# Six chunks of a K-split projection and their conditioning products: another order for the conditioning visits

## The chip, the cores and the metric

The kernel runs on one core of one Trainium2 chip. The metric is device time in microseconds: 1735.44 is the median of three runs (1734.55 to 1738.17).

## The reference, cut to what matters

One decoder layer is computed in float32 for 256 prompt rows and 8 x 4 sample rows, so 288 rows of width 2048, and nine conditioning vectors (one prompt, eight samples).

```python
mod = (jax.nn.silu(c) @ w_ada + b_ada).reshape(N, 1, N_MOD, D)
sh1, sc1, g1, sh2, sc2, g2 = [mod[:, :, i] for i in range(N_MOD)]
h = rmsnorm(x, norm1) * (1 + sc1) + sh1
proj = h @ w_in                       # 2048 -> 10752
...                                   # three gated branches, merged
x = x + g1 * (merged @ w_out)
h2 = rmsnorm(x, norm2) * (1 + sc2) + sh2
x = x + g2 * (jnp.square(jax.nn.relu(h2 @ w_ff1)) @ w_ff2)
```

`proj` cannot start before `sh1` and `sc1` are there for the rows of `h` that it contracts over. Both are products of the conditioning vectors with 2048 x 2048 blocks of `w_ada`, 33.6 MB together.

## The kernel before, in words

Activations lie transposed: 2048 features are 16 tiles of 128 partitions, with 288 columns (rows of x) each. A weight matrix is read in **pieces** of 256 x 512 float32 (512 KB, class `Piece`, load in L246). A piece is split into a high and a low part in a format that TensorE takes at speed (L256 on ScalarE, then L257 on VectorE), and 24 matmuls follow for it (L265 to L267: four blocks of 128 outputs, two k tiles, three products).

All loads of weights go through nine buffers of 512 KB (`rawp`, RAW = 9), in the order of the program, on the queue of SyncE. A buffer of a piece is free once both its splits are done.

The **conditioning visits** (class `AdaFirst`, loads in L146, matmuls in L162) compute `sh1` and `sc1` for a chunk of feature tiles. `ada_first(t0, nt)` makes, for the nt tiles from t0 on, 2 visits where nt is 2 and 4 visits where nt is 4 (two steps each, `per=2`). Each visit has four loads of 512 KB (their rows are 1 KB where nt is 2 and 2 KB where nt is 4) and holds its four buffers until its matmuls are done. The last visit of a chunk is followed by `finish`: the result is copied (L167, ScalarE), transposed (L175, TensorE), summed (L178 and `mod_rows`, VectorE), and `modulated` (L410 to L432, VectorE and ScalarE in turn) makes the two parts of h for this chunk. It is written at a higher priority than the code around it.

The first eight groups of `w_in` (512 outputs each) contract over h in six **chunks** of k tiles, (0,2), (2,2), (4,2), (6,2), (8,4), (12,4). A chunk of two tiles has one piece of each group, so 8 pieces; one of four tiles has 16. So the pieces p0 to p63 in order are: chunk 0 = p0 to p7, chunk 1 = p8 to p15, chunk 2 = p16 to p23, chunk 3 = p24 to p31, chunk 4 = p32 to p47, chunk 5 = p48 to p63. Partial sums are added on VectorE (L303). The visits for chunks 1 to 5 are 2 + 2 + 2 + 4 + 4 = 14, here numbered v0 to v13; v1, v3, v5, v9 and v13 are the last ones of their chunks. Those of chunk 0 (`a0`, eight loads) come ahead of p0.

The list `items` gives the order, and `drive` walks it: before the matmuls of an item it issues the splits of the next two items, and loads as far ahead as nine buffers go. In the kernel before, the visits for chunk c + 1 stand among the pieces of chunk c: L965 puts v0 ahead of p2 and v1 ahead of p5; `interleave` spreads the others over the next chunks, so that v2, v4, v6, v10 stand ahead of the first piece of their stretch, and v9 is three pieces ahead of p32. The visits in the pieces of chunk 3 are v6 ahead of p24, v7 ahead of p26, v8 ahead of p27 and v9 ahead of p29. Among the pieces of chunk 5 and later stand the visits of class `Ada` for the other four parts of `mod` (L203, L215).

Three calls lie in the list too: `load_consts` with `mask_consts` (six loads on SyncE's queue; work on GpSimd) ahead of p26, `prep_states` (transposes L520, L524) ahead of p35, and `prep_sgu` (L511) ahead of p38.

Of the kernel before, what the change touches and what calls it, by code (L numbers as in the profile page):

```python
# [32 lines left out]
def decoder_step(ctx: ExitStack, tc: tile.TileContext, A: dict, O: dict):  # L33
# [151 lines left out]
    def ada_first(t0, nt, per=2):  # L185
        s_ = {}
        return [AdaFirst(s_, t0, nt, list(range(i, i + per))) for i in range(0, 2 * nt, per)]
# [95 lines left out]
    def group(src, n0, kts, rhs, done, krow0=0, width=T):  # L283
        st = {}
        np_ = len(kts) // 2
        return [Piece(st, src, krow0 + i * 256, n0, kts[2 * i:2 * i + 2], rhs, i == 0, i == np_ - 1, done, width)
                for i in range(np_)]

    def chunked(src, n0, rhs, done, chunks):

        part = {}
        last = len(chunks) - 1

        def gather(c):
            def fn(ps):
                if c == 0:
                    part["t"] = atile(F32, (P, 4, T))
                t = part["t"]
                for b in range(4):
                    if c == 0:  # L300
                        S.copy(out=t[:, b, :], in_=ps[b])
                    else:
                        V.tensor_add(out=t[:, b, :], in0=ps[b], in1=t[:, b, :])  # L303
                if c == last:
                    return done([t[:, b, :] for b in range(4)], t)
            return fn

        return [group(src, n0, list(range(t0, t0 + nt)), rhs, gather(c), krow0=t0 * P)
                for c, (t0, nt) in enumerate(chunks)]
# [146 lines left out]
    def x_blocks(b0, b1, move):  # L456
        for b in range(b0, b1):
            acc = bankA()
            for tt, (halves, rows) in enumerate(xs):
                st["pe"] = PE.transpose(out=acc[:, tt * P:tt * P + rows],  # L460
                                        in_=halves[b // 8][:rows, (b % 8) * P:(b % 8 + 1) * P],
                                        identity=ident[:rows, :rows]).ins
            move(out=X[b // 4][:, b % 4, :], in_=acc[:, 0:T])
# [203 lines left out]
    def done_cc(h):  # L667
        def done(ps, _):
            z = gtile((P, 4, WC))
            zs = z[:, :, 2 + TP:WC].rearrange("p b (n k) -> p b n k", k=6)  # L670
            V.memset(z[:, :, 0:2], 0.0)
            for b in range(4):
                G.tensor_copy(out=zs[:, b, :, 0:2], in_=scT[:, 4 * h + b, :].rearrange("p (n k) -> p n k", k=2))
                V.tensor_mul(out=z[:, b, 2:2 + TP], in0=ps[b][:, 0:TP], in1=st["xc"][:, b, 0:TP])
                V.tensor_mul(out=zs[:, b, :, 2:6], in0=ps[b][:, TP:T].rearrange("p (n i) -> p n i", i=TS),
                             in1=st["xc"][:, b, TP:T].rearrange("p (n i) -> p n i", i=TS))
            cv = gtile((P, 4, WC))
            L = WC - 2
            for b in range(4):
                wk = [wcT[:, k * 8 + 4 * h + b:k * 8 + 4 * h + b + 1] for k in range(3)]  # L680
                S.mul(out=cv[:, b, 0:L], in_=z[:, b, 0:L], mul=wk[0])
                V.scalar_tensor_tensor(out=cv[:, b, 0:L], in0=z[:, b, 1:1 + L], scalar=wk[1], in1=cv[:, b, 0:L],
                                       op0=ALU.mult, op1=ALU.add)
                V.scalar_tensor_tensor(out=cv[:, b, 0:L], in0=z[:, b, 2:2 + L], scalar=wk[2], in1=cv[:, b, 0:L],
                                       op0=ALU.mult, op1=ALU.add)
            st["cv", h] = cv
            zt = sp.tile([P, 4, 18], F32, tag="zt", name="zt", bufs=1)
            G.tensor_copy(out=zt[:, :, 0:2], in_=z[:, :, TP:TP + 2])
            for b in range(4):
                G.tensor_copy(out=zt[:, b, 2:18].rearrange("p (n k) -> p n k", k=2), in_=zs[:, b, :, 4:6])  # L690
            return [(4, lambda: conv_tail(h, zt))]
        return done
# [11 lines left out]
    def done_bc(h):  # L704
        def done(ps, _=None):
            cv = st["cv", h]
            cs = cv[:, :, TP:WC - 2 + 0].rearrange("p b (n k) -> p b n k", k=6)
            y = gtile()
            for b in range(4):
                V.tensor_mul(out=y[:, b, 0:TP], in0=ps[b][:, 0:TP], in1=cv[:, b, 0:TP])  # L710
                V.tensor_mul(out=y[:, b, TP:T].rearrange("p (n i) -> p n i", i=TS),
                             in0=ps[b][:, TP:T].rearrange("p (n i) -> p n i", i=TS), in1=cs[:, b, :, 2:6])
            BR[1 + h] = split_act(y)
        return done
# [124 lines left out]
    def done_ff2(q4, j):  # L839
        def done(ps):  # L840
            for b in range(4):
                residual(X[j], j, b, ps[b], 5)
            if q4 < 3:
                return
            add_squares(j)
            xf = gtile()
            for b in range(4):
                S.mul(out=xf[:, b, :], in_=X[j][:, b, :], mul=fnT[:, 4 * j + b:4 * j + b + 1])

            def out_t():  # L850
                for t_, (c0, n) in enumerate(TILES):
                    tp = bankB()
                    for b in range(4):
                        PE.transpose(out=tp[:n, b * P:(b + 1) * P], in_=xf[:, b, c0:c0 + n], identity=ident)  # L854
                    if j % 2 == 0:
                        Y[t_][j // 2] = atile(F32, (P, 1024))
                    (V.tensor_copy if t_ % 2 else S.copy)(out=Y[t_][j // 2][:n, (j % 2) * 512:(j % 2 + 1) * 512],
                                                          in_=tp[:n])
            return [(3, out_t)]
        return done  # L860
# [60 lines left out]
    def interleave(main, extra, tail):  # L921

        out, n, done = [], len(main) - tail, 0
        for i, x in enumerate(main):
            while done < len(extra) and done * n <= i * len(extra):
                out.append(extra[done])
                done += 1
            out.append(x)
        return out + extra[done:]


    chunks = [(0, 2), (2, 2), (4, 2), (6, 2), (8, 4), (12, 4)]
    first = [(OFF_V, done_v), (OFF_XC, done_xc), (OFF_CC, done_cc(0)), (OFF_BC, done_bc(0)), (OFF_U, done_u),
             (OFF_P, done_p), (OFF_XC + 512, done_xc), (OFF_CC + 512, done_cc(1))]
    first = [chunked(w_in, n0, rhs_h, dn, chunks) for n0, dn in first]
    a0 = ada_first(*chunks[0], per=1)
    fill = []
# [3 lines left out]
    def queued(fn):  # L941

        def run():
            with tc.issue_after(st["pe"]):
                return fn()
        return run
# [6 lines left out]
    for it in a0:  # L953
        it.mm = queued(it.mm)
    items = [Call(x_early), a0[0], Call(queued(lambda: x_blocks(7, 9, V.tensor_copy))), a0[1],
             Call(queued(prep_vec)), Call(x_stats), a0[2],
             Call(queued(lambda: x_blocks(9, 10, V.tensor_copy))), a0[3],
             Call(queued(lambda: x_blocks(10, 13, S.copy))), Call(queued(lambda: x_blocks(13, KT, V.tensor_copy)))]
    for c in range(len(chunks)):
        ps_ = [x for g_ in first for x in g_[c]]  # L960
        ex = ada_first(*chunks[c + 1]) if c + 1 < len(chunks) else fill[0:4]
        if c == 0:
            for it in ex:
                it.mm = queued(it.mm)
        mix = ps_[0:2] + ex[0:1] + ps_[2:5] + ex[1:2] + ps_[5:] if c == 0 else interleave(ps_, ex, 2)  # L965
        if c == 3:
            mix = mix[:4] + [Call(mask_consts, load_consts)] + mix[4:]
        if c == 4:
            mix = mix[:4] + [Call(prep_states)] + mix[4:8] + [Call(prep_sgu)] + mix[8:]
        items += mix  # L970

    main = []
    main += group(w_in, OFF_BC + 512, K16, rhs_h, done_bc(1))
# [26 lines left out]
    for q4 in range(4):  # L1000
# [3 lines left out]
        for j in range(4):  # L1004
            g_ = group(w2, j * 512, K16, rhs_f, done_ff2(q4, j), krow0=q4 * D)
# [36 lines left out]
```

## Time and profile before

| what | value |
|---|---|
| median of three runs | 1735.44 us |
| the profiled execution: time, span | 1735.38 us, 1733.6 us |
| TensorE busy | 1703.1 us, 98% |
| VectorE, ScalarE, GpSimd busy | 903.9, 666.5, 135.7 us |
| read from HBM | 360.58 MB, 210 GB/s over the span |

Times in the rows are microseconds from the start of the span. A busy TensorE is one with a matmul under way. The chain of waits is followed back from the last instruction; each row is a stretch of it, with its start, its length, and the engine, tile and line that it spent the time in. Loads of weights are seen in two ways: their issues on SyncE's queue (where the length of a row holds the waiting for buffers between its issues) and the rate of the DMA engines by slices of time.

### The profile page before, as it was taken

What the parts mean: (1) busy time and instruction counts of PE and PEld (TensorE: products, weight loads), DVE (VectorE), ACT (ScalarE), POOL (GpSimd) and SP (SyncE); (2) the same over time, 40 slices, a digit from 0 to 9 for tenths busy, and PEclk for the clock granted to TensorE, in tenths of its full rate; (3) what the DMA queues carried; (4) which work ended last, traced back from release to release, by engine and by line L of the source; (5) the groups of instructions that cost most, each with busy time, mean ns of one, the idle gap of its engine ahead of it and who ended that gap; (6) DMA issues with size and microseconds to landing.
All of it is one profiled execution on the core that took longest, in us unless ns stands there. A gap on an engine that the chain in (4) does not pass through costs nothing.

```text
span 1733.6 us, 30410 instructions
## 1 busy us (share of the span) xinstructions
PE 1703.1 (98%) x12842; PEld 1615.3 (93%) x12842; DVE 903.9 (52%) x1243; ACT 666.5 (38%) x806; POOL 135.7 (8%) x209
## 2 busy tenths in 40 slices
PE   7999999999999999999999999999999999999997
PEld 4997888999999999999999999999999999999997
DVE  3676679534444344455659444445444444445444
ACT  4523344333333333333435333344333443344443
POOL 1000105100000000011310000000000000000011
PEclk9999999999999999999999999999999999999998
DMA  9999876677667766766676645554455544555431
GB/s 301 325 303 327 297 257 227 220 244 238 220 234 255 241 223 230 247 237 225 225 254 234 206 170 160 169 163 166 164 165 170 162 168 164 165 164 165 164 128 55
DMA packets 180847, 365.42 MB, mean 211 GB/s; under 512 B 11932, under 2 KB 29476, under 8 KB 180703
## 3 DMA queue, kind: packets, MB, share of 16 engines
q1 hardware_dynamic: 179735, 362.89, 63.1%
q8 instruction: 100, 1.64, 0.4%
q0 software_dynamic: 976, 0.59, 0.1%
q14 instruction: 36, 0.29, 0.0%
HBM read 360.58 MB, written 3.04 MB: 210 GB/s over the span
## 4 chain that ended last, share of the span: by engine, by line
PE 96%; DVE 1%; DMA 1%; ACT 0%; SPq 0%; issue 0%; POOL 0%; DVEq 0%; ACTq 0%; POOLq 0%
PE acc L265 30%; PE acc L267 30%; PE acc L266 30%; PE misc L215 3%; PE misc L162 2%; DMA raw<-in_w_ada 1%; DVE wl L257 0%; DMA raw<-in_w_in 0%; PE misc L854 0%; PE acc L460 0%; DVE act L897 0%; SPq L72 0%; PE misc L175 0%; ACT wh L256 0%; PE misc L649 0%
## 5 line engine op out<-in xcount | busy, mean ns | idle before, releaser
L265 PE MATMUL acc<-act,wh 128*128 128x288 f32 (+1 forms) x3904 | 1160.0, 297 | 3.3 <-ACT wh L256 2.8
L267 PE MATMUL acc<-act,wl 128*128 128x288 f32 (+1 forms) x3904 | 1154.9, 296 | 3.0 <-DVE wl L257 3.0
L266 PE MATMUL acc<-act,wh 128*128 128x288 f32 (+1 forms) x3904 | 1154.6, 296 | 0.0
L257 DVE TENSOR_TENSOR wl<-raw,wh 128x1024 fp32r<-128x1024 f32 x488 | 619.9, 1274 | 675.4 <-ACT wh L256 674.2
L256 ACT CAST wh<-raw 128x1024 fp32r<-128x1024 f32 x488 | 512.0, 1050 | 950.8 <-PE acc L266 833.4
L265 PEld LDWEIGHTS acc<-act,wh 128*128 128x128 f32 x3904 | 735.9, 189 | 39.4 <-ACT wh L256 26.7
L267 PEld LDWEIGHTS acc<-act,wl 128*128 128x128 f32 x3904 | 736.6, 189 | 3.9 <-DVE wl L257 3.5
L266 PEld LDWEIGHTS acc<-act,wh 128*128 128x128 f32 x3904 | 736.4, 189 | 0.2
L443 POOL TENSOR_TENSOR g<-g,rt 128x32 f32<-128x32 f32 x79 | 34.8, 441 | 861.2 <-DVE rt L441 861.2
L303 DVE TENSOR_TENSOR act<-acc,act 128x288 f32<-128x288 f32 x160 | 68.0, 451 | 31.8 <-PE acc L267 31.3
L215 PE MATMUL misc<-raw,cT 128*32 128x512 f32 x512 | 61.6, 598 | 0.0
L438 DVE SCALAR_TENSOR_TENSOR g<-acc,mod,g 128x256 f32<-128x256 f32 x80 | 38.3, 478 | 44.4 <-PE acc L267 44.4
L736 POOL TENSOR_TENSOR g<-g 128x1152 f32<-128x1152 f32 x8 | 21.3, 2663 | 436.4 <-DVE g L733 436.4
L162 PE MATMUL misc<-raw,cT 128*32 128x256 f32 (+1 forms) x384 | 36.1, 477 | 0.9 <-DMA raw<-in_w_ada 0.9
L215 PEld LDWEIGHTS misc<-raw,cT 128*32 128x32 f32 x512 | 13.4, 109 | 24.2 <-issue 21.4
L371 DVE TENSOR_TENSOR act<-g,act 128x1152 fp32r<-128x1152 f32 (+1 forms) x23 | 35.4, 1540 | 0.6
L733 DVE SCALAR_TENSOR_TENSOR g<-g,acc 128x288 f32<-128x288 f32 x48 | 20.8, 451 | 21.5 <-PE acc L267 21.0
L812 ACT ACTIVATE g<-acc 128x288 f32<-128x288 f32 x56 | 22.8, 408 | 11.0 <-PE acc L267 11.0
L370 ACT CAST act<-g 128x1152 fp32r<-128x1152 f32 (+1 forms) x23 | 26.7, 1161 | 0.9 <-DVE g L650 0.4
L723 ACT ACTIVATE g<-acc 128x288 f32<-128x288 f32 x48 | 19.6, 409 | 12.9 <-PE acc L267 12.9
L162 PEld LDWEIGHTS misc<-raw,cT 128*32 128x32 f32 x384 | 11.4, 113 | 13.7 <-issue 7.5
L813 DVE TENSOR_TENSOR g<-g 128x1152 f32<-128x1152 f32 x14 | 18.9, 1351 | 0.0
(206 smaller groups left out, 400.1 us busy)
## 6 DMA issues: line engine op xcount, KB each, us to landing
raw<-in_w_ff SPq DMA_DIRECT2D x256, 512.0 KB, 3.6
raw<-in_w_ada SPq DMA_DIRECT2D x192, 512.0 KB, 5.8
raw<-in_w_in SPq DMA_DIRECT2D x168, 512.0 KB, 6.1
raw<-in_w_out SPq DMA_DIRECT2D x32, 512.0 KB, 4.2
raw<-in_w_br_conv SPq DMA_DIRECT2D x16, 512.0 KB, 3.7
raw<-in_w_br_pool SPq DMA_DIRECT2D x8, 512.0 KB, 6.2
raw<-in_w_br_sgu SPq DMA_DIRECT2D x8, 512.0 KB, 4.6
act<-in_x_prompt SPq DMA_DIRECT2D x4, 512.0 KB, 7.5
```

The lines of the kernel that those rows point to most:

```text
L162: st["pe"] = PE.matmul(out=acc[32 * j:32 * j + 32, :], lhsT=cT[:, kt, :], rhs=self.w[s, m][:, i, :], start=kt < 2, stop=kt >= KT - 2).ins
L215: PE.matmul(out=acc[32 * j:32 * j + 32, :], lhsT=cT[:, kt, :], rhs=self.w[kt, j // 2][:, (j % 2) * 512:(j % 2 + 1) * 512], start=kt == 0, ...
L256: S.copy(out=self.wh, in_=self.w)
L257: V.tensor_sub(out=self.wl, in0=self.w, in1=self.wh.bitcast(F32))
L265: PE.matmul(out=acc, lhsT=self.wh[:, i, bs], rhs=xh, start=f, stop=False)
L266: PE.matmul(out=acc, lhsT=self.wh[:, i, bs], rhs=xl, start=False, stop=False)
L267: st["pe"] = PE.matmul(out=acc, lhsT=self.wl[:, i, bs], rhs=xh, start=False, stop=l).ins
L303: V.tensor_add(out=t[:, b, :], in0=ps[b], in1=t[:, b, :])
L370: S.copy(out=hi, in_=src)
L371: V.tensor_sub(out=lo, in0=src, in1=hi.bitcast(F32))
L438: V.scalar_tensor_tensor(out=x[:, b, 0:TP], in0=ps[:, 0:TP], scalar=mod[:, mg, kt, 0:1], in1=x[:, b, 0:TP], op0=ALU.mult, op1=ALU.add)
L443: (eng or G).tensor_add(out=x[:, b, TP:T], in0=x[:, b, TP:T], in1=t)
```

## The change

The fourteen visits v0 to v13 become one list. Ahead of piece n (n below 48) stand all visits whose number d, counted from 0, has 1.5 d + 1.5 <= n. The three calls get fixed places, ahead of p28, p36 and p40. The pieces of chunk 5 with the first four `Ada` visits stay as they were. v0 and v1 keep their fence behind the matmuls issued so far (`queued`).

```diff
-    for c in range(len(chunks)):
-        ps_ = [x for g_ in first for x in g_[c]]
-        ex = ada_first(*chunks[c + 1]) if c + 1 < len(chunks) else fill[0:4]
-        if c == 0:
-            for it in ex:
-                it.mm = queued(it.mm)
-        mix = ps_[0:2] + ex[0:1] + ps_[2:5] + ex[1:2] + ps_[5:] if c == 0 else interleave(ps_, ex, 2)
-        if c == 3:
-            mix = mix[:4] + [Call(mask_consts, load_consts)] + mix[4:]
-        if c == 4:
-            mix = mix[:4] + [Call(prep_states)] + mix[4:8] + [Call(prep_sgu)] + mix[8:]
-        items += mix
+    visits = [it for c in range(1, len(chunks)) for it in ada_first(*chunks[c])]
+    for it in visits[0:2]:
+        it.mm = queued(it.mm)
+    extra = {28: [Call(mask_consts, load_consts)], 36: [Call(prep_states)], 40: [Call(prep_sgu)]}
+    pieces = [x for c in range(len(chunks)) for g_ in first for x in g_[c]]
+    last = 4 * chunks[-1][0]
+    done = 0
+    for n, x in enumerate(pieces[0:last]):
+        items += extra.get(n, [])
+        while done < len(visits) and 1.5 * done + 1.5 <= n:
+            items.append(visits[done])
+            done += 1
+        items.append(x)
+    items += interleave(pieces[last:], fill[0:4], 2)
```

## Rows read from the trace of the kernel before

**Rows 1.** The page: busy time by engine, and the chain by engine
```profile
PE 1703.1 (98%) x12842; PEld 1615.3 (93%) x12842; DVE 903.9 (52%) x1243; ACT 666.5 (38%) x806; POOL 135.7 (8%) x209
...
PE 96%; DVE 1%; DMA 1%; ACT 0%; SPq 0%; issue 0%; POOL 0%; DVEq 0%; ACTq 0%; POOLq 0%
```

**Rows 2.** Chain of waits, 0 to 320 us: start, length, what
```profile
39.43 1.86 PE misc L162 x32
...
92.94 1.86 PE misc L162 x32
...
122.79 1.85 PE misc L162 x16
...
144.81 1.92 PE misc L162 x16
146.76 0.59 ACT ev L167
147.40 0.67 PE misc L175 x4
...
152.16 0.40 PE acc L265
...
153.93 0.36 PE misc L520 x2
...
162.36 1.85 PE misc L162 x14
...
175.15 0.59 PE misc L524 x8
...
186.66 0.44 PE misc L511 x4
...
205.17 1.85 PE misc L162 x16
...
208.03 0.44 PE misc L175 x4
...
223.68 1.85 PE misc L215 x16
```

**Rows 3.** Windows by stage: busy time, count, granted clock, DMA share, GB/s
```profile
123.00:162.00 39.00, 35.48 (x263) 27.69 (x256) 25.89 (x56) 11.63 (x15) 0.64 (x1) 1.00 0.96 332
162.00:224.00 62.00, 62.00 (x471) 55.00 (x473) 40.85 (x71) 19.58 (x23) 5.19 (x12) 1.00 0.85 289
```

**Rows 4.** Timeline of ScalarE, 118 to 166 us: start, length, what
```profile
147.24 1.05 ACT L256 CAST wh<-raw 128x1024 fp32r<-128x1024 f32 x1
```

**Rows 5.** Timeline of VectorE, 118 to 166 us
```profile
152.74 0.28 DVE L432 TENSOR_TENSOR act<-g,act 128x128 fp32r<-128x128 f32 x1
152.94 3.48 DVE L257 TENSOR_TENSOR wl<-raw,wh 128x1024 fp32r<-128x1024 f32 x3
```

**Rows 6.** Timeline of SyncE's queue, 0 to 118 us: the first issues of weights
```profile
4.97 13.39 SPq L146 DMA_DIRECT2D raw<-in_w_ada  x8
18.40 2.62 SPq L246 DMA_DIRECT2D raw<-in_w_in  x2
21.12 5.85 SPq L146 DMA_DIRECT2D raw<-in_w_ada  x4
27.07 3.81 SPq L246 DMA_DIRECT2D raw<-in_w_in  x3
33.82 7.57 SPq L146 DMA_DIRECT2D raw<-in_w_ada  x4
```

**Rows 7.** The visits' load, line 146: time from issue to landing
```profile
DMA to landing us min/median/max: 3.7/6.8/11.8
```

**Rows 8.** DMA rate in 40 slices of 18 to 42 us, 0.6 us each
```profile
GB/s 353 343 350 348 348 345 352 347 353 350 376 387 387 377 369 355 355 350 372 328 340 341 357 350 358 374 386 389 386 389 387 364 357 352 350 323 149 55 14 138
```

**Rows 9.** Windows: 138 to 154 us, and the first 20 us
```profile
138.00:154.00 16.00, 12.48 (x87) 9.14 (x84) 10.99 (x28) 5.98 (x10) 0.00 (x0) 1.00 1.04 386
...
0.00:20.00 20.00, 10.60 (x43) 5.05 (x44) 5.08 (x19) 9.77 (x15) 4.58 (x28) 1.00 0.87 265
```

## The prediction

> **What bounds the kernel now.** I read the page first: TensorE is busy 98% of the span and is 96% of the chain that ended last [rows 1]. So a change of order can only win or lose where TensorE waits. Then the chain by stages, between the first conditioning visit and the first `Ada` visit, which starts chunk 5: 39.43 to 223.68 us [rows 2]. Only this stretch changes its order. What TensorE needs there is found from quiet places. From v13 at 205.17 to 223.68 there lie one visit (1.85), one set of transposes (0.44) and five pieces: (18.51 - 1.85 - 0.44) / 5 = 3.24 us for a piece. The stretch holds p2 to p47, so 46 pieces x 3.24 = 149.0, 14 visits x 1.86 = 26.0, and some 3.2 of transposes (L175 five times, L520, L524 and L511 [rows 2]; small ones estimated at half the four-tile ones): 178.2 us. It took 184.25, so 6.1 are waits. Nearly all of it is in one place, behind v9, at 146.76 to 152.16, and the window 123 to 162 shows it as 3.5 us without any matmul [rows 2, 3]. There `finish` goes ahead of the next piece's split: ScalarE casts that piece at 147.24, but VectorE takes its half of the split only at 152.94, after the last instruction of `modulated` [rows 4, 5]. All the rest of the stretch is bound by TensorE, though the transfers are not far behind: 332 GB/s from 123 to 162, 289 from 162 to 224 [rows 3].
>
> **What the change does.** It is said to put each chunk's last visit three pieces ahead of the chunk. The code doesn't. With two steps in a visit there are 14 visits, and the rule 1.5 d + 1.5 <= n puts v0 ahead of p2, v1 of p3, v2 of p5, v3 of p6, and so on to v9 of p15 and v13 of p21. Chunk 4, for which v9 is the last visit, starts at p32, and chunk 5 at p48: the last visits are 5, 10, 15, 17 and 27 pieces ahead. All fourteen now lie within the first 21 pieces, instead of 38 or so, and the 27 pieces p21 to p47 have none. No matmul, split or load is added or removed; what moves is when the bytes are needed.
>
> **Demand against supply.** Two visits and three pieces repeat. They take TensorE 2 x 1.86 + 3 x 3.24 = 13.4 us and need 2 x 4 + 3 = 11 loads of 524,288 bytes, so 5.77 MB: 430 GB/s. What the DMA engines gave when they had all they could take: 349 GB/s in the first ten slices after 18 us, while the 1 KB rows of chunk 0's visits landed, and 386 over the 16 us from 138 on, with pieces and visits of 2 KB rows [rows 8, 9]. A load is then 1.50 us with 1 KB rows and 1.36 with 2 KB rows. So this stretch turns from bound by TensorE to bound by transfers.
>
> **The sum.** Nine buffers let SyncE's queue run ahead only so far. Before v0's matmuls end at 39.43 + 1.86 = 41.29, the kernel before had issued 8 + 2 + 4 + 3 loads and nearly four more [rows 6]. In the new order the loads are 8 of chunk 0, p0, p1, v0's four, p2, v1's four, which is 19; the 20th (p3) is the first that needs a buffer of v0 and goes out at 41.29. Up to the last load of v13 there are 8 + 21 + 56 = 85, so 66 remain: 16 of them (v2 to v5) with 1 KB rows, 50 with 2 KB rows. The first lands 3.7 us after its issue [rows 7], at 45.0; the 65 behind it take 16 x 1.50 + 49 x 1.36 = 90.6. v13 has landed at 135.6, and its matmuls end at 137.5. TensorE alone would have ended v13 at 39.4 + 19 x 3.24 + 14 x 1.86 + 2 = 129, so the transfers cost some 8 us here.
>
> Then v13's `finish`. In the old place of v13 it cost nothing, since the next pieces had been loaded and split before. Now p21 is the load behind v13's, as p29 was behind v9's, and I take what that cost: 5.40 us from the end of the visit to the full run of the next piece, L175's 0.67 among it [rows 2]. The bounds are 0.8 (p21 lands 1.36 after v13 and needs its cast of 1.05 [rows 4], while the visit took 1.86 of that time; a little for the first low half) and 5.4; I take 5.4, the row with the same order of loads. The same chain behind v1, v3, v5 and v9 is costed at nothing, because TensorE waits for loads there anyway and the queue has other buffers to fill; if that cover is gone, each costs up to 3.5 (two tiles, an estimate from half the work of the 5.4) or 5.4 (v9).
>
> Then 27 pieces x 3.24 = 87.5 and 1.5 for L520, L524 and L511, with loads at a third of what the DMA engines can do. Chunk 5 starts at 137.5 + 5.4 + 87.5 + 1.5 = 231.9 instead of 223.68: 8.2 us later. Behind that the order is the old one, and I see nothing that could give it back: chunk 5 is again TensorE with the same `Ada` visits. The three calls move by one or two pieces, and `load_consts` brings its 1.4 MB at a time when the queue is nearly idle instead of one when it carries 332 GB/s; that is hidden by p22 to p27 and costs nothing. The wait behind v9 in the old place is already within the 184.25.
>
> The profiled execution took 1735.38, with 1733.6 in the span, 0.06 off the median of the runs. 1735.4 + 8.2 = 1743.6.
>
> **Which rate holds.** The rows say that 386 GB/s lasted 16 us. The Trainium skill ("DMA: Bandwidth & Descriptors", Specifications) gives about 358 GB/s as the limit of HBM for one core, and 435 for the fabric. By 358 each of the 66 loads would be 1.46 us, an estimate from that page, the sum some 5 us longer and the time 1748; this trace exceeds that limit by 8%, so I don't follow it, but it has never had to keep its rate for 90 us.
>
> **Rivals.**
> (a) *The rate falls to the lowest of the full slices for the whole stretch*, 349 GB/s. For: nothing in the rows lasts 90 us, and freed buffers can come late. Against: 386 for 16 us. Then 66 x 1.50 = 99 instead of 92, +7.3: 1750.9. (This is the side on which the skill's 358 lies.)
> (b) *Every `finish` is exposed*, since each now stands where the next piece has just landed: 3 x 3.5 + 5.4 more would be 1759 at most; a half of it is covered by the waits for loads, 1751. For: [rows 4, 5]. Against: the transfers keep running meanwhile.
> (c) *v13's finish goes behind the splits*, as it did at 208 us, where five pieces ran on at 3.24. Then 137.5 + 0.8 + 87.5 + 1.5 + 0.4 = 227.7, +4.0: 1739.4; with 390 GB/s over all, 2 less, and no difference can be told.
> (d) *Faster: the transfers keep up*, and only the wait behind v9 is gone. Without any wait the stretch takes 178.2, -6.1: 1729.3, for which 430 GB/s are needed. The point from which it decides is v13 landing at 127.4, where the change is even: 66 loads in 84 us, 413 GB/s, or 390 if (c) holds as well. The rows have slices of 389 but no mean above 386. That the change did what it is said to do, with the visits over all 45 pieces, would give the same time; the code excludes it.
> (e) *The granted clock falls* in the new waits. The first 20 us had TensorE busy for 10.60 only, and 138 to 154 for 12.48 of 16, both at 1.00, the 2.4 GHz level [rows 9]; the new stretch is busier than these. If it fell to half, pieces would take 6.5 us, and five of them would already cost 16: 1760.
>
> **Chances and range.** The forecast (transfers bind, v13's finish shows) 0.50; (a) 0.14; (b) 0.11; (c) 0.16; (d) 0.07; (e) 0.02. Some 0.2% or 3.5 us either way can't be told from no change in this kernel: 1732 to 1739. About two thirds of (c) and a tenth of the forecast end there, so 0.16 for no difference; 0.06 for faster; 0.78 for slower. Range: from 1736.5 (between (c) and even) to 1756 (above (a), within (b)).
>
> **What would show it.** SyncE's queue should show v13's loads issued before 136 us and the DMA engines at 350 to 390 GB/s from 45 to 136 without breaks, then about 165. TensorE should wait for L146's loads ahead of v3, v5, v7 and so on, by one to two microseconds each, and have no visit from about 138 to 231. Chunk 5's first L215 should start near 232 instead of 223.68, and all behind it be later by the same. If the DMA rate has gaps in that stretch, the buffers bind and not the engines; if L215 starts before 222, the supply was more than I allow, and the prediction is wrong at its root.

## The result, and the profile after

The changed kernel takes 1753.05 us (median of five runs, 1750.05 to 1756.25) against 1735.44; the ratio is 1.010, 95% interval 1.0087 to 1.0112. It is slower, as forecast, and by 17.6 us instead of 8.2: the time lies inside the range, the loss is twice what was forecast.

First the page of the changed kernel: busy time by engine, and the costliest groups' row of the visits' matmuls (busy us, mean ns of one, idle time before them). Behind it the same row of the kernel before, which had not been shown.

```profile
PE 1714.7 (98%) x12842; PEld 1617.4 (92%) x12842; DVE 904.3 (52%) x1243; ACT 667.3 (38%) x806; POOL 137.0 (8%) x209
...
L162 PE MATMUL misc<-raw,cT 128*32 128x256 f32 (+1 forms) x384 | 43.8, 486 | 0.7 <-DMA raw<-in_w_ada 0.7
```
```profile
L162 PE MATMUL misc<-raw,cT 128*32 128x256 f32 (+1 forms) x384 | 36.1, 477 | 0.9 <-DMA raw<-in_w_ada 0.9
```

The instruction counts are the same, but TensorE is busy for 11.6 us more [rows 1], 7.7 of them in the visits. So not all of the loss is waiting: of the 17.5 us by which the span is longer, 5.9 are. Next the chain of waits of the changed kernel, 0 to 330 us, with v0, v1 and its finish, v7, v9 and its finish, v13, and the first `Ada` visit:

```profile
40.36 1.86 PE misc L162 x32
...
45.62 1.93 PE misc L162 x32
47.63 0.38 ACT ev L167
...
49.29 0.88 DVE g L418 x2
...
51.37 1.15 DVE wl L257
52.56 0.40 PE acc L267
...
97.97 0.97 PE misc L162 x2
101.27 1.85 PE misc L162 x14
...
116.12 1.91 PE misc L162 x14
118.05 0.59 ACT ev L167
...
120.25 1.67 DVE g L418 x4
...
124.12 1.14 DVE wl L257
125.30 0.40 PE acc L267
...
149.62 1.91 PE misc L162 x14
...
242.38 1.85 PE misc L215 x16
```

Read it from behind. Chunk 5 starts at 242.38 instead of 223.68 [rows 2]; from there to the end of the span the two kernels need 1508.7 and 1509.9 us, so everything happens before it. v13 is over at 151.5, and v0 starts at 40.36: 111.2 us, in which TensorE has 89.6 us of work at the prices of the prediction. The window of this way (its length, then TensorE's busy time; the last three columns are the granted clock, the DMA share and GB/s) has 9.5 us without a matmul, and so 12.1 us more with one than those prices give:

```profile
40.30:151.50 111.20, 101.70 (x787) 72.60 (x786) 58.89 (x126) 35.11 (x62) 0.00 (x0) 1.00 0.95 332
```

What stands between is not a wait for the visits' own loads: the chain passes through none of them. Behind v1 and behind v9 it passes through `finish` on VectorE and ScalarE and only then through the low half of the next piece's split (wl): 47.55 to 52.56 and 118.03 to 125.30. In part of that TensorE works on high halves; it is without a matmul for 1.9 us behind v1, 2.5 behind v3, 2.4 behind v5 and 2.5 behind v9, which is nearly all of the 9.5. The next pieces were not late then. The loads of p3 and p4 were issued from 41.40 us on and landed 3.7 and 4.6 us later, ahead of the end of v1 at 47.55; behind v3, v5 and v9 the next piece had landed at 63.2, 81.7 and 114.8, ahead of the visits' ends at 65.6, 84.0 and 118.0. Behind v1 the first of the casts stands on ScalarE behind the copy L167, which waits for the visit (SyncE's row, the landing of its two loads, and two rows of ScalarE):

```profile
41.40 0.88 SPq L246 DMA_DIRECT2D raw<-in_w_in  x2
DMA to landing us min/median/max: 3.7/4.2/4.6
47.63 0.37 ACT L167 COPY ev<-misc 128x256 f32<-128x256 f32 x1 [1.58 <-PE misc L162]
47.90 1.05 ACT L256 CAST wh<-raw 128x1024 fp32r<-128x1024 f32 x1
```

And v7 shows the second thing: its first two records (one matmul) run alone at 97.97, in the middle of a piece, for 0.97 us, and the other 14 at 101.27 for 1.85, what all sixteen take when they run together.

The DMA rate of the changed kernel in 40 slices from 41 to 101 us, 1.5 us each, and the waits of SyncE's queue from 30 to 160 us (line, what it waited for, us in total, times, longest):

```profile
GB/s 16 259 411 338 353 356 352 370 360 345 349 337 132 272 238 320 356 358 354 372 359 350 349 326 136 291 389 306 377 355 389 399 391 385 376 161 15 131 391 400
```
```profile
SPq L246 <- PE misc L162: 39.0, 20, 5.5
SPq L146 <- PE misc L162: 28.9, 8, 6.2
```

The rate is full between, but has a break at 59, at 77 and at 95 us, each behind a last visit (v1, v3, v5) whose finish held TensorE up, and behind v9 one more (46 GB/s from 125 to 126.5 us); the queue stands there for buffers that the next visit's matmuls (L162) have not given back.

### The profile page after: what moved, and what is told of

It reads as the page before. It is cut to its first block, busy times and chain, and to the rows that moved or that the text cites. A ratio compares the mean times of both kernels' runs of the same rounds, so it can differ in the third digit from the quotient of the medians.

```text
span 1751.1 us, 30428 instructions
## 1 busy us (share of the span) xinstructions
PE 1714.7 (98%) x12842; PEld 1617.4 (92%) x12842; DVE 904.3 (52%) x1243; ACT 667.3 (38%) x806; POOL 137.0 (8%) x209
## 4 chain that ended last, share of the span: by engine, by line
PE 94%; DVE 3%; DMA 1%; issue 0%; ACT 0%; SPq 0%; DVEq 0%; ACTq 0%
PE acc L265 29%; PE acc L267 29%; PE acc L266 29%; PE misc L215 3%; PE misc L162 2%; DVE wl L257 1%; DMA raw<-in_w_ada 1%; DMA raw<-in_w_in 1%; DVE g L418 0%; DVE act L303 0%; PE misc L854 0%; DVE act L430 0%; PE acc L460 0%; SPq L72 0%; ACT wh L256 0%
## 5 line engine op out<-in xcount | busy, mean ns | idle before, releaser
L443 POOL TENSOR_TENSOR g<-g,rt 128x32 f32<-128x32 f32 x79 | 34.8, 440 | 861.3 <-DVE rt L441 861.3
L215 PE MATMUL misc<-raw,cT 128*32 128x512 f32 x512 | 61.6, 598 | 0.0
L162 PE MATMUL misc<-raw,cT 128*32 128x256 f32 (+1 forms) x384 | 43.8, 486 | 0.7 <-DMA raw<-in_w_ada 0.7
L215 PEld LDWEIGHTS misc<-raw,cT 128*32 128x32 f32 x512 | 13.4, 109 | 24.2 <-issue 22.5
L162 PEld LDWEIGHTS misc<-raw,cT 128*32 128x32 f32 x384 | 12.5, 115 | 14.7 <-issue 9.3
L301 ACT COPY act<-acc 128x288 f32<-128x288 f32 x32 | 12.8, 399 | 16.5 <-PE acc L267 14.4
```

Source lines behind the costliest of these rows:

```text
L162: st["pe"] = PE.matmul(out=acc[32 * j:32 * j + 32, :], lhsT=cT[:, kt, :], rhs=self.w[s, m][:, i, :], start=kt < 2, stop=kt >= KT - 2).ins
L215: PE.matmul(out=acc[32 * j:32 * j + 32, :], lhsT=cT[:, kt, :], rhs=self.w[kt, j // 2][:, (j % 2) * 512:(j % 2 + 1) * 512], start=kt == 0, ...
L443: (eng or G).tensor_add(out=x[:, b, TP:T], in0=x[:, b, TP:T], in1=t)
```

## The experiments

Kernels are compared by their time, and by one stretch of the chain: from v0's matmuls to the first L215. It leaves out the start, which differed by up to 5.7 us between kernels with the same order there (last section).

| kernel | time, us | ratio to before (interval) | v0 to L215 |
|---|---|---|---|
| before | 1735.44 | | 184.2 |
| changed | 1753.05 | 1.010 (1.0087 to 1.0112) | 202.0 |
| finish later | 1745.26 | 1.0067 (1.0046 to 1.0088) | 197.8 |
| visits whole | 1749.32 | 1.0081 (1.0067 to 1.0094) | 199.0 |
| both | 1743.10 | 1.0045 (1.0030 to 1.0061) | 193.4 |
| half visits | 1748.87 | 1.0084 (1.0064 to 1.0104) | 200.3 |
| half the loads | 1730.93 | 0.9969 (0.9956 to 0.9983) | 179.3 |
| pace 3 | 1734.70 | 0.9995 (0.9985 to 1.0005) | 186.7 |
| pace 3, both | 1733.01 | 0.9980 (0.9971 to 0.9989) | 183.5 |
| pace 2.5, both | 1731.89 | 0.9978 (0.9969 to 0.9988) | 182.8 |
| pace 2.5, both, constants late | 1732.07 | 0.9985 (0.9974 to 0.9996) | 179.8 |
| pace 3, constants late | 1733.70 | 0.9986 (0.9977 to 0.9995) | 179.4 |
| before, constants late | 1728.50 | 0.9960 (0.9948 to 0.9972) | 179.8 |

**Half the loads** (visits of chunks 1 to 5 use one half of their weights twice).

```diff
-                for m in range(2):
+                for m in range(2 if self.t0 == 0 else 1):
...
-                    self.w[i, m] = w
+                    self.w[i, m] = self.w[i, 1] = w
```

> The changed kernel, but each visit loads two blocks of 512 KB instead of four and uses them for both halves of its matmuls (so shift and scale of chunks 1 to 5 come from the same weights); 14.7 MB less is read, visits, matmuls and finish stay where they are. The demand of two visits and three pieces falls from 430 to 7 x 0.524 MB in 13.4 us, 274 GB/s. Theories F and S both say that lateness of the loads is the root: nothing is late, the splits stand ahead of the finish, time 1728 to 1734, no worse than before the change. A third theory P (the dense visits themselves cost TensorE, by finishes on VectorE and ScalarE that come every 18 us, whether loads are late or not): it stays above 1745.

The whole loss goes, and 5 us more. Chain of this kernel, v0 and the first L215:

```profile
39.73 1.86 PE misc L162 x32
...
219.02 1.85 PE misc L215 x16
```

179.3 us is close to what the prediction had for this stretch without any wait (178.2). So the dense visits cost nothing by themselves, theory P is out, and the loads are at the root. Through what, this run doesn't say: the edit halves the bytes, and also the buffers that a visit holds, and the order of the instructions came out another. Here ScalarE has p3's cast at 42.93 us, ahead of v1's copy L167 at 46.92.

**Finish later.**

```diff
-                    self.finish(ev)
-            return []
+                    self.end = [(2, queued(lambda: self.finish(ev)))] if self.t0 else self.finish(ev) or []
+            return getattr(self, "end", [])
```

> The changed kernel, but the finish of v1, v3, v5, v9 and v13 is issued behind the matmuls of the next two items instead of at once; loads, order of visits and pieces stay. Theory F (finish stands ahead of the splits of pieces that landed late, on VectorE and ScalarE, and that is where TensorE's 18 us went): TensorE waits at most 2 us behind each last visit, the time falls by 9 to 14 us to 1739 to 1744, and the breaks in the DMA rate close. Theory S (the supply binds: nine buffers and the DMA engines give no more than about 330 GB/s in this order): TensorE waits at other places for the same bytes, the time stays within 4 us of 1753.

1745.26: 7.8 us less, below the 9 to 14 of theory F, and 3.6 of them are an earlier start (v0 at 36.73, the first L215 at 234.56 in its chain). In the stretch it brings 4.2. Neither theory is confirmed. TensorE's waits did not shrink: from v0 to the end of v13 it is without a matmul for 9.3 us (rows under **Both**) instead of 9.5. What shrank is its busy time, of which line 162 has 39.7 us instead of 43.8. The edit leaves the copy L167 where it was.

**Visits whole.**

```diff
-    for it in visits[0:2]:
+    for it in visits:
```

> The changed kernel with all fourteen visits fenced behind the matmuls issued before them (queued), not only v0 and v1; finish, loads and places stay. In the changed kernel the first matmul of a late visit is issued alone in the middle of the piece before it and costs TensorE 0.55 or 0.97 us instead of its share of 1.86; line 162 is busy for 43.8 us there and 36.1 before. Theory O (this split order costs its 7.7 us of TensorE): line 162 back to 36 us and the time down by 4 to 8, to 1745 to 1749. Theory S (the supply binds, the split visits only fill time that TensorE would wait in): line 162 back to 36 us and the time within 3 us of 1753.

Line 162 is back to 36.8 us, and the time 3.7 less, 3.0 in the stretch: short of the 4 to 8 of theory O. The profiled execution took 1752.29, with v0 late, at 42.4 us. TensorE also lost its clock in it, behind v9. Windows of 5 us; the third column from the right is the granted clock:

```profile
115.00:120.00 5.00, 2.19 (x16) 1.50 (x12) 3.28 (x13) 3.50 (x7) 0.00 (x0) 0.99 1.04 383
120.00:125.00 5.00, 3.76 (x14) 3.42 (x15) 4.21 (x8) 1.69 (x3) 0.00 (x0) 0.50 1.02 378
```

Held up behind v9 (busy for 2.19 of the 5 us in the first row), it then ran at 0.50, the lower of its two levels (1.2 GHz), and a matmul of a piece took 0.6 us instead of 0.3. In the changed kernel no window of 5 us between 40 and 170 us is below 1.00.

**Both.**

> The changed kernel with both: visits fenced as in the run beside it, finish behind the next two items. If finish and split order are all of the loss, 1731 to 1738. If the bytes bind below them, with 66 loads in the stretch at the 350 GB/s that the DMA engines reached once finish was out of the way, it comes out where the run with finish alone did, 1742 to 1746, whatever line 162 does.

1743.10, inside the second expectation. TensorE's timeline gives v0, v13 and the first L215; then the DMA rate in 40 slices from 41 to 143 us, 2.55 us each:

```profile
39.91 1.93 PE L162 MATMUL misc<-raw,cT 128*32 128x256 f32 x32
...
140.51 1.92 PE L162 MATMUL misc<-raw,cT 128*32 128x512 f32 x16
...
233.31 1.92 PE L215 MATMUL misc<-raw,cT 128*32 128x512 f32 x16
```
```profile
GB/s 152 385 354 351 365 349 353 372 355 348 364 352 348 294 361 393 319 305 401 311 339 387 379 369 390 380 386 363 392 389 387 331 300 402 388 374 386 386 386 389
```

There are no breaks left but dips: 36.56 MB in the 102 us, 358 GB/s. It looks like the kernel that the prediction described, bound by the rate of the transfers, but TensorE's waits say otherwise. The windows from v0 to the end of v13, of finish later, both, and half the loads (length, then TensorE's busy time):

```profile
36.70:143.80 107.10, 97.83 (x787) 72.22 (x786) 58.88 (x126) 35.20 (x62) 0.00 (x0) 1.00 1.02 354
39.85:142.40 102.55, 92.69 (x787) 71.50 (x786) 58.79 (x126) 35.22 (x62) 0.00 (x0) 1.00 1.02 356
39.70:130.60 90.90, 90.74 (x788) 71.28 (x788) 59.48 (x130) 37.39 (x65) 1.60 (x1) 1.00 0.86 285
```

With both edits the way takes 102.5 us instead of 111.2. The 8.7 us are busy time, most of it line 162's, which has 36.0 instead of 43.8. TensorE is still without a matmul for 9.9 us, and 6.2 of them lie directly behind v1, v3, v5 and v9, where it waits for a cast. Behind v1 (TensorE, then ScalarE):

```profile
48.61 0.40 PE L265 MATMUL acc<-act,wh 128*128 128x288 f32 x1 [1.52 <-ACT wh L256]
47.24 0.37 ACT L167 COPY ev<-misc 128x256 f32<-128x256 f32 x1 [1.57 <-PE misc L162]
47.51 2.00 ACT L256 CAST wh<-raw 128x1024 fp32r<-128x1024 f32 x2
```

The pieces of these casts had landed by 45.9, before v1 ended at 47.1; the casts stand behind the copy again. So the 11.7 us that are left against half the loads (90.8, 39.73 to 130.55) are not the supply's alone. How much of them is, and whether the engines' rate or the nine buffers set it, no run shows; one with more buffers was not made.

**Half visits** (`per=1`, twice as many visits of half the size at twice the pace: the same bytes ahead of the same pieces).

> The changed kernel with one step in a visit instead of two (28 visits of two loads each) at 0.75 d + 1.5 <= n, so that the same bytes are wanted ahead of the same pieces, but a visit holds two buffers, not four, and gives them back earlier. If the holding of four buffers is what starves the queue: 1738 to 1745 and a DMA rate above 350 GB/s from 45 to 140 us. If finish ahead of late splits is the cause, or the engines' rate, it stays within 4 us of 1753.

4.2 us less, 1.7 in the stretch, between the two expectations. It can't be read as one cause: there are more split visits (line 162 is busy for 50.3 us; TensorE has a matmul under way for 111.3 of the 111.9 us to the end of the last visit), and the rate from 41 to 155 us is 341 GB/s against 334. That the size of a visit isn't the main thing is likely by this, not shown.

**Pace 3**, which is what the change was said to do, and the same with finish later and visits whole (the three edits above; the last of the three runs has 2.5 in place of 3).

```diff
-        while done < len(visits) and 1.5 * done + 1.5 <= n:
+        while done < len(visits) and 3 * done + 1.5 <= n:
```

> The changed kernel with 3 d + 1.5 <= n in place of 1.5 d + 1.5 <= n: what the change is said to do, last visits at most five pieces ahead and v9 three ahead of its chunk. One visit and three pieces need 7 loads in 1.86 + 9.72 = 11.6 us, 317 GB/s. If the demand above the supply is the cause, TensorE runs through and even the 5 us behind v9 of the kernel before go: 1728 to 1733. If even this pace is too dense for nine buffers, 1736 to 1742.

> Pace 3 d + 1.5 with visits fenced and finish behind the next two items. 317 GB/s are wanted, so the supply is no matter. The run at pace 3 alone lost about 5 us behind v9 (finish ahead of late splits) and 1 to 2 in split visits, and was no faster than before the change; with both gone: 1728 to 1731, faster than both kernels by 0.3%. If the loss behind v9 has another cause, 1733 to 1736.

> As the run beside it with 2.5 d + 1.5: one visit and two and a half pieces want 3.41 MB in 1.86 + 8.1 us, 342 GB/s, just under the 350 or so that the queue reached at pace 1.5. If the supply is a limit at about 350, this still runs through, 1728 to 1733; if nine buffers give less than 340 in steady use, 1735 to 1739.

Pace 3 alone is the same as before; my 1728 to 1733 was wrong. The wait behind v9 was still there. With finish later and visits whole, 3 and 2.5 are both faster than the kernel before by 0.2%, but neither reaches the 179 us of the run with half the loads. The longer waits of TensorE in the three kernels (in brackets the idle time before the instruction, and what ended it; the second kernel has two rows):

```profile
153.51 0.40 PE L265 MATMUL acc<-act,wh 128*128 128x288 f32 x1 [2.77 <-DVE act L303]
161.09 0.66 PE L524 MATMUL misc<-ident,g 16*128 16x16 f32 x8 [1.53 <-DVE spT L521]
162.22 0.63 PE L511 MATMUL misc<-ident,g 128*128 128x128 f32 x4 [0.47 <-DVE scT L525]
143.39 0.40 PE L267 MATMUL acc<-act,wl 128*128 128x288 f32 x1 [1.77 <-DVE wl L257]
```

The first and the last stand behind v9's `modulated` on VectorE, the two between behind copies of `prep_states` there. After each of them the clock fell: it was granted at 0.72 from 155 to 160 us in the first kernel, 0.79 from 165 to 170 in the second and 0.71 from 145 to 150 in the third. The constants (`load_consts`, 1.4 MB) are issued at 121 to 133 us in these kernels, shortly ahead of the pieces behind v9.

**Constants late**, in three kernels; here as edited in the kernel before. The edit moves all three calls behind the last visit: `load_consts` with `mask_consts`, `prep_states` and `prep_sgu`.

```diff
-        if c == 3:
-            mix = mix[:4] + [Call(mask_consts, load_consts)] + mix[4:]
         if c == 4:
-            mix = mix[:4] + [Call(prep_states)] + mix[4:8] + [Call(prep_sgu)] + mix[8:]
+            mix = mix[:15] + [Call(mask_consts, load_consts)] + mix[15:]
+        if c == 4:
+            mix = mix[:19] + [Call(prep_states)] + mix[19:20] + [Call(prep_sgu)] + mix[20:]
```

> The kernel before the change, with load_consts and mask_consts moved from p26 to p43 (behind v13), prep_states to p46 and prep_sgu to p47; nothing else. If the 1.4 MB ahead of v7 to v9 are what made p29 late, and so put finish ahead of its split, the 5 us behind v9 go: 1729 to 1731. If v6 to v9 are late by their own bytes (24 loads in 33 us, 380 GB/s), the wait stays: 1733 to 1736.

> Pace 2.5 d + 1.5 with visits fenced and finish behind the next two items as before, and load_consts (six loads, 1.4 MB) with mask_consts moved from p28 to p42, where no visit is left, prep_states to p46 and prep_sgu to p47. At pace 2.5 the wait that is left stands at 138 to 150 us, where these loads share the queue with v9's and v10's. If they make the pieces behind them late, 3 to 4 us go: the way from v0 to the first L215 falls from 182.8 to 179 to 180 us, the time to 1728 to 1730. If the wait is finish alone, nothing changes: 1731 to 1733.

> Pace 3 d + 1.5 alone (no fence, finish at once), with the same three calls at p42, p46 and p47. Same question as beside it: if the 1.4 MB make the pieces behind v9 late, the way from v0 to the first L215 falls from 186.7 to about 180, the time to 1728 to 1731; if finish ahead of the split costs its 5 us wherever a last visit stands, 1733 to 1736.

All three have the stretch at 179.4 to 179.8. In the kernel before, v9 and v11 were 33.4 us apart (144.81 [rows 2] and 178.21); with the constants late, by its chain, 27.8 (some 1.2 of the difference are the transposes of `prep_states`, which only moved):

```profile
178.21 1.85 PE misc L162 x16
```
```profile
143.96 1.85 PE misc L162 x16
...
171.78 1.85 PE misc L162 x16
...
218.40 1.85 PE misc L215 x16
```

The kernel before with this one edit takes 1728.50, ratio 0.996 (0.9948 to 0.9972): the best of all, and faster than both. What in the edit does it is not shown. On SyncE's queue only three of the six loads went late (560 KB); the other three (768 KB) still go out ahead of v9:

```profile
117.14 0.48 SPq L495 DMA_DIRECT2D sgn<-in_sgu_norm  x1
...
119.74 0.47 SPq L496 DMA_DIRECT2D wgp<-in_w_pool_grp  x1
120.25 0.50 SPq L497 DMA_DIRECT2D bsg<-in_b_sgu  x1
...
184.90 0.46 SPq L490 DMA_DIRECT2D g<-in_w_sgu  x1
185.58 0.36 SPq L492 DMA_DIRECT2D g<-in_state_pool  x1
186.00 0.45 SPq L494 DMA_DIRECT2D g<-in_state_conv  x1
```

v9 starts 105.4 us behind v0 in both kernels, and p29 lands 1.1 us sooner against v0. In the kernel before it was issued at 137.93 and landed 7.3 us later, at 145.2, while v9 was still running. The order on ScalarE differs: there p29's cast (147.24 [rows 4]) stands behind v9's copy, with the calls late ahead of it (one row of the kernel before, two of the other):

```profile
146.76 0.59 ACT L167 COPY ev<-misc 128x512 f32<-128x512 f32 x1 [8.09 <-PE misc L162]
```
```profile
143.34 1.05 ACT L256 CAST wh<-raw 128x1024 fp32r<-128x1024 f32 x1 [6.91 <-DMA raw<-in_w_in]
145.91 0.59 ACT L167 COPY ev<-misc 128x512 f32<-128x512 f32 x1 [1.51 <-PE misc L162]
```

The other two kernels gain the same in the stretch and lose it again in chunk 5, so their times miss what was expected: from the first L215 to the end of the span they take 1513 to 1514 us instead of 1509 to 1510 (TensorE busy for 34.8 and 33.8 of the 40 us from 260 to 300, against 37.3 in the kernel before with the constants late). Both wait 4.3 us there for a low half on VectorE, the third 2.7, and the clock falls: from 295 to 300 us it is granted at 0.50 with pace 2.5, 0.67 with pace 3 and 0.66 in the third. What is late there was not tried.

## Why the prediction was right in direction and wrong in size

**The reading of the code, and the demand, held.** The visits are done by p21, 430 GB/s are wanted, the kernel gets 332 on this way, chunk 5 starts late, and everything behind it is late by the same. With half of the loads taken out the loss is gone, and with pace 3, as the change was said to be, nothing is lost. That the engines' rate sets the time is not shown. TensorE did not wait for the loads of v3, v5 and v7, where one to two microseconds each were said, and the rate had gaps, for which the prediction itself says that the buffers bind and not the engines. So the direction is right because of the loads, as forecast, but the way from the loads to the lost time is another than the forecast's.

**The step that failed** is the sentence that the finish chain "behind v1, v3, v5 and v9 is costed at nothing, because TensorE waits for loads there anyway and the queue has other buffers to fill". It was not covered. TensorE did not wait for the visits' loads at all; behind v1, v3, v5 and v9 it was without a matmul for 9.3 us together, for casts and low halves that stood behind `finish` although the next piece had landed. And the queue did not have other buffers: those of the next visit were full and not used, so the transfers stood too, at 59, 77, 95 and 125 us. The prediction let a wait of TensorE and one of the transfers hide each other; here the one is followed by the other. No run took these waits away alone: finish later and both left 9.3 and 9.9 us, so what they cost in the whole time is argued from the profile. Rival (b) was nearest to this, at 1751 with a half covered; it had a chance of 0.11.

**A term that was not in the prediction**: the visits came apart, with the first matmul of a visit alone in the middle of the piece before it. That is 7.7 us of TensorE by line 162; with the visits whole the time fell by 3.7, and by 2.2 with finish later. What puts the matmul there is not shown.

**The rate term is open.** The 65 loads were put at 90.6 us, 376 GB/s. The best that a kernel with all the loads reached on this way is 358, with both edits, some 4.5 us more; but TensorE's waits held buffers back there too, so this is not what the engines can give at most. The Trainium skill ("DMA: Bandwidth & Descriptors", Specifications) has 358 as the limit of HBM for a core, the rule that was set aside. The slices show that it is a mean here and no cap: about 350 while 1 KB rows are loaded, 386 to 392 in many of the later ones.

**A term that was too large**: v13's finish, 5.4 us. From the end of v13 to the first L215 the sum had 94.4 us; it took 90.85, where half the loads takes 88.5. VectorE has low halves of the pieces behind v13 at 154.77, 156.66 and 158.61 us, ahead of its `modulated` (161.20). The 5.4 was itself more than a wait: TensorE worked on high halves in it and was without a matmul for 3.5 us.

The sum from forecast to measurement, 231.9 to 242.4 us for chunk 5: start +0.9, v0 to v13 +13.1 (8.7 of it go with finish later and visits whole, 4.4 stay), v13's finish -3.5. Behind chunk 5 it took 1.2 less than before.

**The wait behind v9 in the kernel before** was put down to `finish` ahead of a late split. That is where it showed. With the three calls moved it is gone, so it hangs on where they stand; whether through the bytes of the constants or through the order of the instructions is open. The prediction moved them in passing, at no cost, which was right (TensorE is never without a matmul in the changed kernel from 167 us to the first L215), and did not see what they did where they stood.

## What to carry to other kernels

When a change moves loads without adding any, work out the demand of the repeating pattern and set it against the rate that the transfers reach when they are never held up; here 430 against the 349 and 386 of the rows said which way it goes. Then don't let one wait hide another: what holds up the engine that frees the buffers also stops the transfers a little later, as the breaks behind v1, v3, v5 and v9 show. A piece that has landed is no use until its cast is reached: look at what stands ahead of it on its engine. And ahead of reordering the large transfers, look at which small calls stand among them: moving three brought more than any pace.

## What was not expected of the hardware

- The first matmuls of the span run at one of two speeds. Sixteen records of line 162 with 256 columns took 1.94 us in the changed kernel and 1.07 in the one with finish later, at the same place of the same order, with the granted clock's column at 1.00 in both (TensorE's timeline, one row of each):

```profile
19.86 1.94 PE L162 MATMUL misc<-raw,cT 128*32 128x256 f32 x16
```
```profile
18.56 1.07 PE L162 MATMUL misc<-raw,cT 128*32 128x256 f32 x16
```

  v0 started between 36.7 and 42.4 us over the kernels. What decides it is open (in visits whole, where v0 was the latest, the clock was granted at 0.70 from 35 to 40 us); it is why a stretch that begins at v0 is compared here, and not the spans.
- A single matmul of a visit of 512 columns, which fills one of four column groups, took 0.97 us, and eight of them in turn on all four groups 1.85.
